# Values projected with 512 moving columns in two units ahead of the attention, and one filling tile per head

## The chip, the cores and the metric

The kernel runs on one core of one Trainium2 chip. A core has five engines with their own instruction streams: TensorE (PE: matmul, with its weight loads listed as PEld), VectorE (DVE), ScalarE (ACT), GpSimd (POOL) and SyncE (SP, which here issues most of the loads). The metric is the device time of one execution in microseconds (us).

## What is computed

One trunk layer on x of 512 tokens by 1024 features, all in float32 (cut to what matters here):

```python
xn = rmsnorm(x, g)
u = xn @ W_in                       # columns: q | k | v | rnn_x | rnn_gate | gate_A | gate_B, 1024 each
# A: 16 heads of 64; a query of chunk c reads the keys of chunks c-8 .. c (chunks of 64 tokens)
s = q @ k.T / 8 + bias[head, clipped distance];  s = where(valid, s, -1e30)
o = softmax(s) @ v
# B: causal convolution of width 4 -> RG-LRU scan, times gelu(rnn_gate)
yA, yB = o @ W_attn_out, B @ W_rnn_out
h = x + (sigmoid(gate_A) * yA + sigmoid(gate_B) * yB) @ W_o
h = h + (silu(hn @ W_g) * (hn @ W_u)) @ W_ffn_out     # hn = rmsnorm(h)
out = rmsnorm(h)
```

## The kernel before

**Products.** A value of float32 is kept as a pair of fp32r numbers, high part and rest. `mm3` (L71 to L78) makes one product of pairs with three matmuls: high by high (L76), high by low (L77), low by high (L78). `split` (L82, L83) makes a pair: ACT copies the high part out of the source, DVE subtracts it from the source. The stationary side of a matmul has 128 columns; the moving side has up to 512, and the result fills up to 512 columns of one PSUM bank. There are eight banks: four for tiles of the kind "mm", two for "t", two for "s".

**Weights.** `plan` lists chunks of weights in the order in which they are loaded. SP loads them into a ring of raw buffers, and `weights(name)` returns a chunk as pairs and has the next one in the list split by ACT and DVE while PE uses this one.

**Stages.** The norm; then the projections of branch B and the gates; then q and k of the first pair of heads (`q_tile(0)`, `k_tile(0)`); then the stage in question; then `po_ya` (the attention's way out), the merge, `w_o` and the feed-forward part.

**Projections for attention.** Two heads share one tile of q and one of k (128 features by 512 tokens): 24 matmuls of 128x512 each, `project` calling `mm3` for eight slices of the features. `q_tile` (L834) evicts with two ACT (L841) and two DVE instructions (L842). `k_tile` (L845) evicts each half with ACT (L852), DVE (L853), ACT (L854), all reading the same bank, and POOL copies the low half (L855). Four heads share one group of values, 256 columns of the weights. `v_tile(group, t)` (L868) makes the values of 128 tokens: the tokens are the stationary side, the 256 weight columns the moving side, 24 matmuls of 128x256; one split evicts it.

**A head.** `scores(h)` (L879) makes four blocks of scores with eight matmuls (L895, L896) into an "s", an "mm" and an "s" bank; DVE adds the bias and takes the maximum (L904), ACT takes the exponential and its sum (L905), DVE the reciprocal (L906), POOL multiplies (L910; the widest block goes to DVE in some heads). `transposed(h)` (L913) turns the blocks with ten matmuls (L921) into two "t" banks and an "mm" bank, and three splits evict them. `weigh(h)` (L930) multiplies by the values with eight matmuls (L941) into an "mm" bank; ACT (L942) and DVE (L943) evict, and each second head splits the pair's result.

**Order.** In front of the loop: the four `v_tile`s of group 0, then eight tiles `po_yb` of branch B's way out, with `scores(0)` after the sixth. In the loop (L964 to L983) PE's order is the order of the program: the transposes of head h, the scores of head h + 1, filling tiles, the weighing of head h, further filling tiles. `laid(h)` (L953) is the table of the filling tiles: from head 0 to 11 it spreads the q and k tiles of later pairs and the values of the next group, three or four narrow tiles beside or in place of a wide one; heads 12 to 15 have one tile of gate A each. The other engines' order in this stage is made by a scheduler.

Of the kernel before, what the change touches and what calls it, by code (L numbers as in the profile page):

```python
# [8 lines left out]
F32 = mybir.dt.float32  # L9
F32R = mybir.dt.float32r  # L10
# [4 lines left out]
P = 128  # L15
D = 1024
S = 512
KT = D // P
NT = S // P
HEADS = 16  # L20
HD = 64
# [17 lines left out]
def block_kernel(ctx: ExitStack, tc: tile.TileContext, x, norm_mix_g, w_in, b_merge, rel_table,  # L39
# [31 lines left out]
    def mm_tile(name, tag="mm"):  # L71
        return ps.tile([P, S], F32, tag=tag, bufs=4 if tag == "mm" else 2, name=name)

    def mm3(o, sh, sl, mh, ml, start, stop, parts=False):

        pe.matmul(o, sh, mh, start=start, stop=False, skip_group_check=parts)  # L76
        pe.matmul(o, sh, ml, start=False, stop=False, skip_group_check=parts)  # L77
        pe.matmul(o, sl, mh, start=False, stop=stop, skip_group_check=parts)  # L78

    def split(hi, lo, src):  # L80

        act.activation(hi, src, AF.Copy)  # L82
        dve.tensor_sub(lo, src, f(hi))  # L83
# [5 lines left out]
    def cols(src, col, width=CW):  # L89
        return (src, col, width)  # L90
# [16 lines left out]
    def plan_qk(pr):  # L107
        plan(f"qk{pr}", cols(w_in, C_Q + pr * P, P), cols(w_in, C_K + pr * P, P))

    def plan_v(gr):  # L110
        plan(f"v{gr}", cols(w_in, C_V + gr * CW))

    plan_qk(0)
    plan_v(0)
    for j in range(0, KT, 2):
        plan(f"yb{j}", cols(w_rnn_out, j * P))
    for pr in range(1, HEADS // 2):
        plan_qk(pr)
        if pr in (2, 4, 6):
            plan_v(pr // 2)  # L120
    for j in (4, 6):
        plan(f"ga{j}", cols(w_in, C_GA + j * P))
    for j in range(0, KT, 2):
# [212 lines left out]
    def weights(name, ahead=1):  # L336
        prefetch(index[name] + 1 + ahead)
        if index[name] + 1 == len(made):
            low_parts()
        return made[index[name]]  # L340
# [431 lines left out]
        return po  # L772


    zs = [[zp.tile([P, 2, S], F32, name=f"z{w}{j}") for j in range(0, KT, 2)] for w in "ab"]
    ta, zB = ([t[j // 2][:, j % 2] for j in range(KT)] for t in zs)
# [57 lines left out]
    def q_tile(pr):  # L834
        po = mm_tile(f"po_q{pr}")
        project(po, weights(f"qk{pr}"), 0, xnT)
        q = qk_pool(pr).tile([P, 2, S], F32R, tag="qk", bufs=3, name=f"q{pr}")
        for e in range(2):
            own, other = halves(e)
            src = backwards(po[own, :])  # L840
            act.activation(blocks(q[own, e]), src, AF.Copy, scale=0.125)  # L841
            dve.scalar_tensor_tensor(blocks(q[other, e]), src, 0.125, blocks(f(q[own, e])), ALU.mult, ALU.subtract)  # L842
        qk[pr] = [q]

    def k_tile(pr):  # L845
        po = mm_tile(f"po_k{pr}")
        project(po, weights(f"qk{pr}"), 1, xnT)
        kh = qk_pool(pr).tile([P, 2, S], F32R, tag="qk", bufs=3, name=f"kh{pr}")
        kl = qk_pool(pr).tile([P, 2, S], F32R, tag="qk", bufs=3, name=f"kl{pr}")
        for e in range(2):  # L850
            own, other = halves(e)
            act.activation(kh[own, e], po[own, :], AF.Copy)  # L852
            dve.tensor_sub(kl[own, e], po[own, :], f(kh[own, e]))  # L853
            act.activation(kh[other, e], po[own, :], AF.Copy)  # L854
            pool.tensor_copy(kl[other, e], kl[own, e])  # L855
        qk[pr] += [kh, kl]
# [8 lines left out]

    vs = {}

    def v_tile(gr, t):  # L868
        wv = weights(f"v{gr}")
        po = mm_tile(f"po_v{gr}_{t}", "mm" if gr else "t")  # L870
        for k in range(KT):
            mm3(po[:, 0:256], xnT[k][:, 0, t * P:(t + 1) * P], xnT[k][:, 1, t * P:(t + 1) * P],
                wv(0, k, whole), wv(1, k, whole), k == 0, k == KT - 1)
        v = aw.tile([P, 2, 4, HD], F32R, tag="v", bufs=8, name=f"v{gr}_{t}")
        split(v[:, :, 0::3], v[:, :, 1:3], po[:, 0:256].rearrange("p (a b d) -> p a b d", a=2, b=2))
        vs.setdefault(gr, []).append(v)


    def scores(h):  # L879
        pr, e = divmod(h, 2)  # L880
        q, kh, kl = qk[pr]
        bias = bias_tile(h)
        lsum = cp.tile([P, NT], F32, tag="lsum", bufs=2, name=f"l{h}")
        nmax = cp.tile([P, NT], F32, tag="nmax", bufs=2, name=f"m{h}")
        rl = cp.tile([P, NT], F32, tag="rl", bufs=2, name=f"rl{h}")
        prob = [aw2.tile([P, (qb + 1) * P], F32, tag=f"p{qb}", name=f"p{h}_{qb}") for qb in range(NT)]

        low = ps.tile([P, S], F32, tag="s", bufs=2, name=f"s{h}_01")
        scs = [low[:, 0:P], low[:, 256:512], mm_tile(f"s{h}_2"), ps.tile([P, S], F32, tag="s", bufs=2, name=f"s{h}_3")]

        def products(qb):
            w = (qb + 1) * P
            sc = scs[qb][:, 0:w]
            qs = q[:, e, qb * P:(qb + 1) * P]
            pe.matmul(sc, qs, kh[:, e, 0:w], start=True, stop=False, skip_group_check=qb < 2)  # L895
# [10 lines left out]
        dve.reciprocal(rl[:], lsum[:])  # L906
        for qb in range(NT):

            eng = dve if qb == NT - 1 and h % 4 == 1 and h > 1 else pool
            eng.tensor_scalar(prob[qb][:], prob[qb][:], rl[:, qb:qb + 1], 1.0, ALU.mult, ALU.mult)  # L910
        return prob

    def transposed(h, prob):  # L913

        pp = [aw2.tile([P, 2, S], F32R, tag="pt", bufs=4, name=f"pp{h}_{i}") for i in range(3)]
        for i, kbs in enumerate(((0,), (1,), (2, 3))):
            pt = mm_tile(f"pT{h}_{i}") if i == 2 else ps.tile([P, S], F32, tag="t", bufs=2, name=f"pT{h}_{i}")
            for kb in kbs:
                for qb in range(kb, NT):
                    at = qb - min(kb, 2) if kb < 3 else 2  # L920
                    pe.transpose(pt[:, at * P:(at + 1) * P], prob[qb][:, kb * P:(kb + 1) * P], ident[:])  # L921
            n = (512, 384, 384)[i]
            split(pp[i][:, 0, 0:n], pp[i][:, 1, 0:n], pt[:, 0:n])
        return pp
# [25 lines left out]

    def laid(h):  # L953
        m, at = divmod(h, 4)
        qs, ks, va = (lambda pr: lambda: q_tile(pr)), (lambda pr: lambda: k_tile(pr)), (lambda t: lambda: v_tile(m + 1, t))
        if h >= 12:
            return [lambda: gate(0, h - 8)], []
        first_, second = 2 * m + 2, 2 * m + 3
        return {0: (([qs(1), ks(1)] if m == 0 else []) + ([] if m == 0 else [qs(first_)]), [qs(first_)] if m == 0 else []),
                1: ([ks(first_)], [va(0)]),  # L960
                2: ([va(1), va(2)], [va(3)]),
                3: ([qs(second)], [ks(second)])}[at]

    for t in range(NT):  # L964
        v_tile(0, t)
# [394 lines left out]
```

## Time and profile before

| what | us |
|---|---|
| median of three runs | 867.02 (867.0 to 867.12) |
| span of the profiled execution | 865.5 |
| first values matmul to first `po_ya` matmul | 185.23 to 431.14 |
| transposes of head 0 | 241.60 |

The profile lists, for one execution, what each engine did and when. The span runs from the first to the last instruction; it is the profiled execution's own time and lies 1.5 us below the median of the runs. Matmuls are pipelined on PE, so the listed length of one overlaps the next; the distance between two starts says what one costs. In the views by windows each row is one stretch: its limits and length, then the busy time of PE, PEld, DVE, ACT and POOL with the number of instructions, then the clock granted to TensorE (1.00 is full speed), the share of time in which the DMA engines were busy, and GB/s. In a timeline row the first number is the start, the second the length; in square brackets stands the idle time of the engine ahead of it and what ended it. In the list of waits of an engine the numbers are the total, how often, and the longest.

### The profile page before, as it was taken

The numbers are of one execution on the slowest core, as the hardware profiler recorded it, in microseconds if no ns is written. First come the engines' busy times: TensorE is split into PE (matmuls) and PEld (weight loads), VectorE is DVE, ScalarE is ACT, GpSimd is POOL, SyncE is SP. The second block draws the span as 40 slices with busy tenths as digits, with TensorE's granted clock in tenths as the row PEclk, the third lists the DMA queues.
The fourth block names the chain that finished last, engine by engine and source line by source line (L and its number), as shares of the span: only waits on it lengthen the run. The fifth ranks groups of instructions, "written<-read, shape, count | busy, mean of one in ns | idle before, by whom it ended". The sixth has DMA issues, their size and how long they took to land.

```text
span 865.5 us, 13353 instructions
## 1 busy us (share of the span) xinstructions
PE 856.4 (99%) x5130; PEld 761.1 (88%) x5130; DVE 600.9 (69%) x950; ACT 498.1 (58%) x878; POOL 95.2 (11%) x161
## 2 busy tenths in 40 slices
PE   9999999999999999999999999999999999999997
PEld 6988888888889889898888889999999999888885
DVE  5666656573456585766556556988888888698885
ACT  6595747752356585767633357555555556545434
POOL 2412111120112132221200000000000001000000
PEclk9999999999999999999999999999999999999999
DMA  9133232433323332232223712424333332437542
GB/s 289 57 119 106 68 120 76 123 98 98 109 88 95 81 103 74 81 113 64 74 76 121 266 51 72 145 79 131 109 98 98 99 98 85 148 100 227 185 134 97
DMA packets 88767, 96.39 MB, mean 111 GB/s; under 512 B 5784, under 2 KB 74992, under 8 KB 88704
## 3 DMA queue, kind: packets, MB, share of 16 engines
q1 hardware_dynamic: 87072, 92.03, 34.3%
q10 hardware_dynamic: 1232, 2.95, 0.9%
q8 instruction: 40, 0.66, 0.3%
q0 software_dynamic: 400, 0.57, 0.2%
q14 instruction: 23, 0.19, 0.1%
HBM read 93.39 MB, written 2.14 MB: 110 GB/s over the span
## 4 chain that ended last, share of the span: by engine, by line
PE 97%; DVE 1%; ACT 1%; DMA 0%; issue 0%; ACTq 0%; DVEq 0%
PE po_out L76 2%; PE po_out L77 2%; PE po_out L78 2%; PE o L941 2%; PE p_fu L78 2%; PE p_fg L78 2%; PE p_fg L77 2%; PE p_fg L76 2%; PE p_fu L76 2%; PE p_fu L77 2%; PE pT L921 2%; PE po_v L76 2%; PE po_v L78 2%; PE po_v L77 2%; PE po_gb L76 2%; PE po_xr L77 2%
## 5 line engine op out<-in xcount | busy, mean ns | idle before, releaser
L910 POOL TENSOR_SCALAR p<-p,rl 128x128 f32<-128x128 f32 (+3 forms) x61 | 34.9, 590 | 135.7 <-DVE rl L906 135.4
L905 ACT ACTIVATE p<-p,m 128x128 f32<-128x128 f32 (+1 forms) x64 | 35.7, 560 | 11.0 <-DVE m L904 10.8
L76 PE MATMUL po_v<-whl_v,xnT 128*128 128x256 f32 x128 | 36.5, 285 | 0.0
L78 PE MATMUL po_v<-whl_v,xnT 128*128 128x256 f32 x128 | 36.2, 283 | 0.0
L77 PE MATMUL po_v<-whl_v,xnT 128*128 128x256 f32 x128 | 36.2, 283 | 0.0
L1131 POOL TENSOR_TENSOR act_lo<-act,act_hi 128x1024 fp32r<-128x1024 f32 x1 | 2.4, 2405 | 300.7 <-ACT act_hi L1130 300.7
L76 PE MATMUL po_out<-whl_fo,act_hi 128*128 128x512 f32 (+1 forms) x80 | 30.8, 385 | 0.5 <-ACT c_u L370 0.5
L78 PE MATMUL po_out<-whl_fo,act_lo 128*128 128x512 f32 (+1 forms) x80 | 30.7, 384 | 0.0
L77 PE MATMUL po_out<-whl_fo,act_hi 128*128 128x512 f32 (+1 forms) x80 | 30.7, 384 | 0.0
L904 DVE CUSTOM_DVE_ANT_0 p<-s,bias 128x128 f32<-128x128 f32 (+1 forms) x64 | 29.1, 483 | 1.0 <-PE s L896 1.0
L83 DVE TENSOR_TENSOR whl_qk<-raw_qk,whl_qk 128x1024 fp32r<-128x1024 f32 x16 | 20.5, 1284 | 13.2 <-ACT whl_qk L82 13.0
L83 DVE TENSOR_TENSOR whl_fu_s<-s_fu,whl_fu_s 128x1024 fp32r<-128x1024 f32 x20 | 24.1, 1222 | 6.2 <-ACT whl_fu_s L82 6.2
L77 PE MATMUL po_xr<-xnT,whl_xr 128*128 128x512 f32 (+1 forms) x80 | 27.7, 353 | 0.0
L83 DVE TENSOR_TENSOR pp<-pT,pp 128x384 fp32r<-128x384 f32 (+1 forms) x48 | 27.5, 596 | 0.1
L77 PE MATMUL po_gr<-xnT,whl_gr 128*128 128x512 f32 (+1 forms) x80 | 27.5, 347 | 0.0
L78 PE MATMUL po_gr<-xnT,whl_gr 128*128 128x512 f32 (+1 forms) x80 | 27.3, 347 | 0.0
L78 PE MATMUL po_xr<-xnT,whl_xr 128*128 128x512 f32 (+1 forms) x80 | 27.2, 346 | 0.0
L76 PE MATMUL po_gr<-xnT,whl_gr 128*128 128x512 f32 (+1 forms) x80 | 27.2, 347 | 0.0
L83 DVE TENSOR_TENSOR whl_fg_s<-s_fg,whl_fg_s 128x1024 fp32r<-128x1024 f32 x20 | 24.0, 1222 | 4.1 <-ACT whl_fg_s L82 4.0
L76 PE MATMUL po_xr<-xnT,whl_xr 128*128 128x512 f32 (+1 forms) x80 | 26.3, 351 | 0.4 <-ACT xnT L566 0.4
L82 ACT ACTIVATE whl_qk<-raw_qk 128x1024 fp32r<-128x1024 f32 x16 | 16.8, 1053 | 17.0 <-PE po_yb L78 10.4
L76 PE MATMUL po_gb<-xnT,whl_gb 128*128 128x512 f32 x64 | 25.2, 394 | 0.0
(487 smaller groups left out, 3247.5 us busy)
## 6 DMA issues: line engine op xcount, KB each, us to landing
raw_fg<-in_w_ffn_in_dram SPq DMA_DIRECT2D x24, 512.0 KB, 4.2
raw_fu<-in_w_ffn_in_dram SPq DMA_DIRECT2D x22, 512.0 KB, 3.9
raw_qk<-in_w_in_dram SPq DMA_DIRECT2D x32, 256.0 KB, 3.2
raw_fo<-in_w_ffn_out_dram SPq DMA_DIRECT2D x16, 512.0 KB, 3.6
raw_xr<-in_w_in_dram SPq DMA_DIRECT2D x8, 512.0 KB, 4.3
raw_gr<-in_w_in_dram SPq DMA_DIRECT2D x8, 512.0 KB, 3.6
raw_ga<-in_w_in_dram SPq DMA_DIRECT2D x8, 512.0 KB, 4.7
raw_gb<-in_w_in_dram SPq DMA_DIRECT2D x8, 512.0 KB, 3.5
```

Source lines behind the costliest of these rows:

```text
L76: pe.matmul(o, sh, mh, start=start, stop=False, skip_group_check=parts)
L77: pe.matmul(o, sh, ml, start=False, stop=False, skip_group_check=parts)
L78: pe.matmul(o, sl, mh, start=False, stop=stop, skip_group_check=parts)
L82: act.activation(hi, src, AF.Copy)
L83: dve.tensor_sub(lo, src, f(hi))
L904: dve.tensor_tensor_reduce(prob[qb][:], scs[qb][:, 0:w], bias[:, S - w:S], -1.0, 3e38, ALU.add, ALU.min, nmax[:, qb:qb + 1])
L905: act.activation(prob[qb][:], prob[qb][:], AF.Exp, bias=nmax[:, qb:qb + 1], scale=-1.0, accum_out=lsum[:, qb:qb + 1])
L910: eng.tensor_scalar(prob[qb][:], prob[qb][:], rl[:, qb:qb + 1], 1.0, ALU.mult, ALU.mult)
L921: pe.transpose(pt[:, at * P:(at + 1) * P], prob[qb][:, kb * P:(kb + 1) * P], ident[:])
L941: pe.matmul(po[:, S - n:S], st, pp[i][:, part, lo:lo + n], start=kb == 0 and part == 0, stop=kb == NT - 1 and part == 1)
L1131: (dve if i else pool).tensor_sub(lo[:], o[:], f(hi[:]))
```

## The change

The values of all four groups are now made ahead of the loop, in two units of two groups each: (0, 3) and (1, 2). A unit has 512 moving columns, 256 of each group, and four PSUM banks at once, one for each block of 128 tokens. It takes its weights in two chunks, each with half of the features and 512 columns. PE goes through two slices of the features for one bank (six matmuls), then to the next bank. Each bank is evicted by two splits, one for each group. The groups 0 and 3 lie in the buffers that values had before; group 1 lies in a buffer of the ring that later takes the pairs of attention results, and group 2 in two buffers that later take gate A's last tiles (`z_tiles`).

In front of the loop now stand `v_unit(0)`, the eight `po_yb` tiles with `scores(0)` after the sixth, `q_tile(1)`, `k_tile(1)`, `v_unit(1)` and `scores(1)`. In the loop each head has one filling tile, right behind its transposes, and then come the scores of head h + 2.

```diff
-    def plan_v(gr):
-        plan(f"v{gr}", cols(w_in, C_V + gr * CW))
+    v_groups = ((0, 3), (1, 2))
+
+    def plan_v(u):
+        for kh in range(2):
+            plan(f"v{u}_{kh}", *(cols(w_in, C_V + gr * CW) for gr in v_groups[u]), rows=kh * S, kts=KT // 2)
...
-    for pr in range(1, HEADS // 2):
+    plan_qk(1)
+    plan_v(1)
+    for pr in range(2, HEADS // 2):
         plan_qk(pr)
-        if pr in (2, 4, 6):
-            plan_v(pr // 2)
...
-    def v_tile(gr, t):
-        wv = weights(f"v{gr}")
-        po = mm_tile(f"po_v{gr}_{t}", "mm" if gr else "t")
-        for k in range(KT):
-            mm3(po[:, 0:256], xnT[k][:, 0, t * P:(t + 1) * P], xnT[k][:, 1, t * P:(t + 1) * P],
-                wv(0, k, whole), wv(1, k, whole), k == 0, k == KT - 1)
-        v = aw.tile([P, 2, 4, HD], F32R, tag="v", bufs=8, name=f"v{gr}_{t}")
-        split(v[:, :, 0::3], v[:, :, 1:3], po[:, 0:256].rearrange("p (a b d) -> p a b d", a=2, b=2))
...
+    def v_unit(u):
+        po = [mm_tile(f"po_v{u}_{t}") for t in range(NT)]
+        for kh in range(2):
+            wv = weights(f"v{u}_{kh}")
+            for kk in range(0, 4, 2):
+                for t in range(NT):
+                    toks = slice(t * P, (t + 1) * P)
+                    for k in (kk, kk + 1):
+                        xk = xnT[4 * kh + k]
+                        mm3(po[t][:], xk[:, 0, toks], xk[:, 1, toks], wv(0, k, every), wv(1, k, every),
+                            kh == k == 0, kh == 1 and k == 3)
+        homes = [v_homes(gr) for gr in v_groups[u]]
+        for t in range(NT):
+            for n, gr in enumerate(v_groups[u]):
+                v = homes[n][t]
+                v = v[:] if gr in v_groups[0] else v
+                split(v[:, :, 0::3], v[:, :, 1:3],
+                      po[t][:, n * CW:(n + 1) * CW].rearrange("p (a b d) -> p a b d", a=2, b=2))
...
-    def laid(h):
-        m, at = divmod(h, 4)
...
+    def fill(h):
         if h >= 12:
-            return [lambda: gate(0, h - 8)], []
...
+            if h % 2 == 0:
+                z_tiles("a", (h - 8,))
+            return gate(0, h - 8)
+        (k_tile if h % 2 else q_tile)(2 + h // 2)
+
+    v_unit(0)
+    probs = {}
     for j in range(KT):
         if j == 6:
-            prob = scores(0)
+            probs[0] = scores(0)
...
+    q_tile(1)
+    k_tile(1)
+    v_unit(1)
+    probs[1] = scores(1)
     with tc.manual_schedule(engines={mybir.EngineType.PE}):
         for h in range(HEADS):
-            pp = transposed(h, prob)
-            if h + 1 < HEADS:
-                prob = scores(h + 1)
-            before, after = laid(h)
-            for what in before:
-                what()
+            pp = transposed(h, probs.pop(h))
+            fill(h)
+            if h + 2 < HEADS:
+                probs[h + 2] = scores(h + 2)
             weigh(h, pp)
-            for what in after:
-                what()
```

How PE's order stands before and after, at three places. In these rows a name carries a buffer number at its end; `po_v0_2` is the PSUM tile of group (before) or unit (after) 0 for the tokens of block 2, `whl_...` is the split weight. The first place is PE at the start of the values, before:

```order
L78 MATMUL po_k0_1669<-xnT_155,whl_qk0_4_1571 128x512
L76 MATMUL po_v0_0_1722<-whl_v0_0_1630,xnT_155 128x256
...
L76 MATMUL po_v0_0_1722<-whl_v0_4_1635,xnT_155 128x256
...
L76 MATMUL po_v0_1_1750<-whl_v0_0_1630,xnT_155 128x256
```

and after the change, each row being the first of six matmuls or more on the same bank (the fourth bank's tile, `po_v0_3`, comes 38 matmuls behind the first):

```order
L76 MATMUL po_v0_0_1712<-whl_v0_0_0_1628,xnT_155 128x512
...
L76 MATMUL po_v0_1_1713<-whl_v0_0_0_1628,xnT_155 128x512
...
L76 MATMUL po_v0_2_1714<-whl_v0_0_0_1628,xnT_155 128x512
...
L76 MATMUL po_v0_0_1712<-whl_v0_0_2_1634,xnT_155 128x512
...
L76 MATMUL po_v0_0_1712<-whl_v0_1_0_1716,xnT_155 128x512
L77 MATMUL po_v0_0_1712<-whl_v0_1_0_1716,xnT_155 128x512
L76 MATMUL po_v0_3_1715<-whl_v0_0_0_1628,xnT_155 128x512
```

Before, one narrow tile ran through all 24 matmuls on one bank; now four banks take turns, and the fourth begins late.

The second place is PE in head 5 (`pT` are the transposes, `s` the scores, `o` the weighing), before:

```order
L921 MATMUL pT5_0_2859<-ident_119,p5_0_2776 128x128
...
L895 MATMUL s6_01_2888<-kh3_2738,q3_2695 128x128
...
L76 MATMUL po_k4_2912<-xnT_155,whl_qk4_0_2659 128x512
...
L941 MATMUL o5_2947<-pp5_0_2856,v1_0_2447 128x512 x2
...
L76 MATMUL po_v2_0_2973<-whl_v2_0_2805,xnT_155 128x256
...
L921 MATMUL pT6_0_3004<-ident_119,p6_0_2884 128x128
```

and after the change, with the semaphores that the rows wait for:

```order
L953 MATMUL pT5_0_2940<-ident_119,p5_0_2786 128x128 [waits PE_49,Pool_49]
...
L76 MATMUL po_k4_2959<-xnT_155,whl_qk4_0_2636 128x512 [waits DVE_49]
...
L927 MATMUL s7_01_3004<-kh3_2770,q3_2672 128x128
...
L973 MATMUL o5_3028<-pp5_0_2937,v1_2343 128x512 [waits DVE_49,Activation_49]
...
L953 MATMUL pT6_0_3045<-ident_119,p6_0_2897 128x128 [waits PE_49,Pool_49]
...
L76 MATMUL po_q5_3064<-xnT_155,whl_qk5_0_2850 128x512 [waits DVE_49]
```

The k tile of pair 4 moved ahead of the scores, the scores are those of head 7 where they were those of head 6, the values tile behind the weighing is gone, and the q tile that follows in head 6 waits for DVE.

More of the change, by code (lines that the diff above doesn't have):

```diff
@@ L772, in tile_of, with z_tiles @@
         return po
-    zs = [[zp.tile([P, 2, S], F32, name=f"z{w}{j}") for j in range(0, KT, 2)] for w in "ab"]
-    ta, zB = ([t[j // 2][:, j % 2] for j in range(KT)] for t in zs)
+    def z_tiles(w, js):
+        for j in js:
+            late = w == "a" and j >= 4
+            t = zp.tile([P, 2, S], F32, tag="late" if late else f"z{w}{j}", bufs=2 if late else 1, name=f"z{w}{j}")
+            for c in range(2):
+                (ta if w == "a" else zB)[j + c] = t[:, c]
+    ta, zB = {}, {}
+    z_tiles("a", (0, 2))
+    z_tiles("b", range(0, KT, 2))
     def gate(w, j):
@@ L866, in block_kernel, with v_homes @@
     vs = {}
-    def v_tile(gr, t):
-        wv = weights(f"v{gr}")
-        po = mm_tile(f"po_v{gr}_{t}", "mm" if gr else "t")
-        for k in range(KT):
-            mm3(po[:, 0:256], xnT[k][:, 0, t * P:(t + 1) * P], xnT[k][:, 1, t * P:(t + 1) * P],
-                wv(0, k, whole), wv(1, k, whole), k == 0, k == KT - 1)
-        v = aw.tile([P, 2, 4, HD], F32R, tag="v", bufs=8, name=f"v{gr}_{t}")
-        split(v[:, :, 0::3], v[:, :, 1:3], po[:, 0:256].rearrange("p (a b d) -> p a b d", a=2, b=2))
-        vs.setdefault(gr, []).append(v)
+    def v_homes(gr):
+        if gr in v_groups[0]:
+            return [aw.tile([P, 2, 4, HD], F32R, tag="v", bufs=8, name=f"v{gr}_{t}") for t in range(NT)]
+        if gr == v_groups[1][0]:
+            big = rnp.tile([P, 2, 2, S], F32R, tag="big", bufs=4, name=f"v{gr}")
+            rows = [big[:, t // 2, t % 2] for t in range(NT)]
+        else:
+            pairs = [zp.tile([P, 2, S], F32R, tag="late", bufs=2, name=f"v{gr}_{n}") for n in range(2)]
+            rows = [pairs[t // 2][:, t % 2] for t in range(NT)]
+        return [o.rearrange("p (a b d) -> p a b d", a=2, b=4) for o in rows]
+    def v_unit(u):
[16 more added lines that the diff above has]
+                      po[t][:, n * CW:(n + 1) * CW].rearrange("p (a b d) -> p a b d", a=2, b=2))
+                vs.setdefault(gr, []).append(v)
     def scores(h):
@@ L949, in weigh @@
             aT.append(o)
-    def laid(h):
-        m, at = divmod(h, 4)
-        qs, ks, va = (lambda pr: lambda: q_tile(pr)), (lambda pr: lambda: k_tile(pr)), (lambda t: lambda: v_tile(m + 1, t))
+    def fill(h):
         if h >= 12:
-            return [lambda: gate(0, h - 8)], []
[L958 to L965, printed above, removed]
+            if h % 2 == 0:
[4 more added lines that the diff above has]
+    probs = {}
     for j in range(KT):
         if j == 6:
-            prob = scores(0)
+            probs[0] = scores(0)
         po = mm_tile(f"po_yb{j}")
```

## The prediction

> **What bounds the kernel now.** I read the busy times of the engines first, then the chain of waits that ended last, then what PE (TensorE) waited for over the whole program.
>
> ```profile
> PE 856.4 (99%) x5130; PEld 761.1 (88%) x5130; DVE 600.9 (69%) x950; ACT 498.1 (58%) x878; POOL 95.2 (11%) x161
> PE 97%; DVE 1%; ACT 1%; DMA 0%; issue 0%; ACTq 0%; DVEq 0%
> PE busy L396 <- DVE eps_t L402: 1.2, 1, 1.2
> PE pt_mix_0t L564 <- DVE xs_mix L544: 0.6, 2, 0.4
> PE po_out L76 <- ACT c_u L370: 0.5, 1, 0.5
> PE po_xr L76 <- ACT xnT L566: 0.4, 2, 0.2
> ```
>
> PE is busy for 856.4 of the 865.5 us, 97% of the chain is PE, and its listed waits (the last four rows: total, times, longest) belong to the warm-up, the first norm, the first projection and the last stage. None names a tile of the attention. The windows over the stretch that the change touches, from the first values matmul to the last head's end, say the same; two more of them serve below.
>
> ```profile
> 185.23:241.60 56.37, 56.37 (x297) 48.70 (x296) 23.22 (x34) 18.39 (x28) 5.12 (x8) 1.00 0.33 98
> 241.60:431.14 189.54, 189.54 (x1129) 169.33 (x1128) 125.84 (x273) 125.81 (x273) 44.76 (x84) 1.00 0.30 86
> 348.27:366.42 18.15, 18.15 (x102) 15.86 (x100) 13.81 (x33) 14.42 (x33) 4.75 (x9) 1.00 0.30 88
> 405.19:414.27 9.08, 9.08 (x53) 7.92 (x52) 5.38 (x14) 6.35 (x15) 3.30 (x6) 1.00 0.01 3
> 742.15:745.80 3.65, 3.65 (x18) 3.01 (x17) 3.25 (x3) 1.33 (x2) 0.00 (x0) 1.00 0.38 140
> ```
>
> The columns are length, then busy us of PE, PEld, DVE, ACT and POOL, then the granted clock, the DMA share and GB/s. PE fills both stretches to the last digit (56.37 of 56.37, 189.54 of 189.54) at a clock of 1.00. So there is no wait in here to remove: only less PE work can shorten it, and any new PE wait lengthens it one for one.
>
> **The term that shrinks: values at half the instructions.** A busy time on PE overlaps its neighbours, so I price by spacing of starts, not by the mean duration.
>
> ```profile
> L76 PE MATMUL po_v<-whl_v,xnT 128*128 128x256 f32 x128 | 36.5, 285 | 0.0
> 174.35 0.39 PE L76 MATMUL po_q<-xnT,whl_qk 128*128 128x512 f32 x1
> 185.23 0.28 PE L76 MATMUL po_v<-whl_v,xnT 128*128 128x256 f32 x1
> 275.92 0.28 PE L76 MATMUL po_v<-whl_v,xnT 128*128 128x256 f32 x1
> 281.67 0.40 PE L941 MATMUL o<-pp,v 128*128 128x512 f32 x1
> ```
>
> Between 174.35 and 185.23 stand the 48 wide matmuls of q0 and k0: 10.88/48 = 0.2267 us each. Between 275.92 and 281.67 stand the 48 narrow ones of two values tiles: 5.75/48 = 0.1198 us. The difference, 0.1069 us for 256 more columns, is 0.418 ns a column; what is left of the narrow one, 0.1198 − 0.1069 = 0.0129 us, is paid once per matmul whatever its width. The values take 3 × 128 = 384 narrow matmuls now and 192 wide ones after, so 384 × 0.1198 = 46.0 us become 192 × 0.2267 = 43.5 us: **2.5 us less**. The row 742.15:745.80 shows wide matmuls in the shape of the new unit, whose PSUM bank changes after every six:
>
> ```profile
> 742.15 0.40 PE L76 MATMUL po_out<-whl_fo,act_hi 128*128 128x512 f32 x1
> 743.54 0.39 PE L76 MATMUL po_out<-whl_fo,act_hi 128*128 128x512 f32 x1
> 744.90 0.39 PE L76 MATMUL po_out<-whl_fo,act_hi 128*128 128x512 f32 x1
> ```
>
> They start 1.39 and 1.36 us apart, 0.232 and 0.227 us per matmul. With 0.232 throughout the unit would cost 1.0 us more; with the 0.2267 of the long stretch, nothing. I take the 0.2267, since the second group is already back at it, and keep a gain of 1.5 to 2.5 us. The trace has no wide matmul with tokens as the stationary and weights as the moving side; its worst would be twice the narrow spacing, 0.2396 us, at which the gain is 0.
>
> Here the Trainium skill speaks against the change: TensorE: Matmul & The Clock Gate, section Back-to-back issue gap, gives an isolated warm matmul N/2.4 + 2.5 ns. By its 2.5 ns the saving would be 192 × 2.5 ns = 0.5 us, an estimate from that page, and the time about 866.5 us. The trace's 12.9 ns is five times that, and it also disagrees with the same section's sustained 131 ns for N=512, being 227 ns here; I go by the trace.
>
> **What moves at no PE work.** Outside that, PE does the same matmuls in another order: per head ten transposes, one filling tile, eight score matmuls, eight weighing matmuls. The seams between kinds could cost. A head of that content exists already, with scores ahead of the filler (head 13), and one with the filler straight behind the transposes (head 15, which has no scores left):
>
> ```profile
> 405.19 1.28 PE L921 MATMUL pT<-ident,p 128*128 128x128 f32 x10
> 407.59 0.40 PE L76 MATMUL po_ga<-xnT,whl_ga 128*128 128x512 f32 x1
> 413.06 1.37 PE L941 MATMUL o<-pp,v 128*128 128x512 f32 x8
> 423.34 1.28 PE L921 MATMUL pT<-ident,p 128*128 128x128 f32 x10
> 424.38 0.48 PE L76 MATMUL po_ga<-xnT,whl_ga 128*128 128x512 f32 x1
> 429.93 1.37 PE L941 MATMUL o<-pp,v 128*128 128x512 f32 x8
> 431.14 0.44 PE L76 MATMUL po_ya<-aT,whl_ya 128*128 128x512 f32 x1
> 229.43 0.22 PE L895 MATMUL s<-kh,q 128*128 128x128 f32 x1
> 230.70 0.40 PE L76 MATMUL po_yb<-rnn,whl_yb 128*128 128x512 f32 x1
> ```
>
> Head 15 gives transposes 1.04, filler 5.55, weighing 1.21; scores behind wide matmuls took 230.70 − 229.43 = 1.27. The sum for the new order is 9.07 us, against 9.08 for head 13. So the seams are worth 0, with ±0.05 a head over 14 heads, ±0.7 us, kept for the range.
>
> **What the other engines are asked.** The scores of a head now come two heads ahead of its transposes. Softmax ends on POOL:
>
> ```profile
> 411.21 3.02 POOL L910 TENSOR_SCALAR p<-p,rl 128x128 f32<-128x128 f32 x4 [5.23 <-DVE rl L906]
> ```
>
> These end at 414.23, and the next head's transposes start at 414.27 (407.59 + 5.47 + 1.21): just in time, with the scores one head ahead. Two heads ahead they have another 9.07 us. Since PE did not wait for them, that is worth 0 now, but it is the cover for the rest: from the end of the scores (407.59) to POOL's end (414.23) lie 6.64 us, and the new place of the scores behind the filler leaves only the weighing's 1.21 us between them and the next transposes. With scores one head ahead in that place PE would lose 5.4 us a head.
>
> The new order has one q or k tile in every head from 0 to 11. The window 348.27:366.42 is exactly such a pair, two heads with one k and one q tile between them: ACT 14.42 and DVE 13.81 of 18.15 us, 79% and 76%, and PE did not wait. It holds a weight split of values that the new loop lacks, so the new loop is not denser than this. The narrow values' evictions, four for every four heads, leave the loop too and go to the two units in front:
>
> ```profile
> L82 ACT ACTIVATE v<-po_v x16: 361/384/385, 189.1 to 381.8; 128x256 fp32r<-128x256 f32 x16
> L83 DVE TENSOR_TENSOR v<-po_v,v x16: 417/424/427, 189.9 to 382.6; 128x256 fp32r<-128x256 f32 x16
> ```
>
> A unit holds four banks and each needs two of these pairs: 2 × 0.384 + 0.424 = 1.19 us. Within a unit the banks finish one after the other, 6 × 0.2267 = 1.36 us apart, so the first is free 4.08 − 1.19 = 2.9 us ahead of the unit's end and the last 1.19 us behind it. What follows wants banks of that kind one by one. Worth 0; if ACT were held up until a unit's end, each unit would cost one bank's 1.19 us, 2.4 us for both. At the front the unit needs four banks at once and the k tile ahead of it holds one; the built order starts the fourth tile only after 38 matmuls, 8.6 us into the unit.
>
> Loads: the same bytes in the same half-megabyte portions, 3 of the 4 MB of values weights earlier, past the later q and k loads on SP's queue, in stretches where the DMA share is 0.33 and 0.30. Worth 0; weights are split one chunk ahead as before.
>
> **The sum.** 865.5 − 2.5 + 0 = 863.0 us of span. The median of the runs shown, 867.02, is 1.5 above the span, which I carry over: **864.5 us**. The low end is 0.7 less by seams (863.8); the high end takes the seams the other way (865.2).
>
> **The rivals.**
>
> *A: k-tile evictions become the stop (slower).* A k tile is evicted half by half, each on one bank in series ACT, DVE, ACT:
>
> ```profile
> L852 ACT ACTIVATE kh<-po_k x16: 591/593/596, 185.8 to 399.7; 64x512 fp32r<-64x512 f32 x16
> L853 DVE TENSOR_TENSOR kl<-po_k,kh x16: 682/686/695, 187.2 to 402.4; 64x512 fp32r<-64x512 f32 x16
> 348.47 0.59 ACT L852 ACTIVATE kh<-po_k 64x512 fp32r<-64x512 f32 x1 [1.67 <-PE po_k L78]
> 348.96 1.04 ACT L82 ACTIVATE whl_v<-raw_v 128x1024 fp32r<-128x1024 f32 x1
> 355.28 0.60 ACT L854 ACTIVATE kh<-po_k 64x512 fp32r<-64x512 f32 x1 [0.49 <-DVE kl L853]
> ```
>
> Dense, that is 4 × 0.593 + 2 × 0.686 = 3.74 us, and with one weight split (1.04) ahead of it in ACT's queue 4.8; in the trace it stretched from 348.47 to 355.88, 7.4 us, since nobody waited. From a k tile's end to the next filler PE has scores, weighing and transposes, 1.27 + 1.21 + 1.04 = 3.5 us. If the next filler takes the k tile's bank, PE loses at least 1.3 us, and 3.9 by the stretched chain. I take 1.5 in six heads, 9 us: 864.5 + 9 = 873.5. For it: the order now puts fillers closer to evictions than before. Against it: the built program makes the filler behind a k tile wait on DVE alone, which is the reader of a score tile; the k tile's last reader is ACT. It decides if the banks go round so that a filler meets the k tile's own.
>
> *B: the gain is eaten (no change).* Either the two evictions show, 864.5 + 2.4 = 866.9, or the wide form with moving weights runs at the bound of 0.2396 us, which gives 867.0; the skill's rule above is its mild form. For it: that form is not in the trace. Against it: the narrow form moves weights as well, and PEld, which loads the stationary side, is busy for 88% against PE's 99%, so the loads are hidden as they stand.
>
> *C: the clock.* If the units' bank changes made the granted clock drop to half, each wide matmul would cost 512 × 0.418 ns = 0.214 us more: 192 × 0.214 = 41 us, about 905. Against it: 742.15:745.80 changes banks the same way at 1.00. The Trainium skill, same page, section A second HAM failure mode: psum-queue depth-cycling, tells of such an oscillation when banks are cycled; this trace disagrees at that place, with its 1.00.
>
> *D: "two heads ahead" brings a gain of its own.* There is none to bring: PE has no idle time in 241.60:431.14.
>
> **How the numbers follow.** Forecast 0.70, B 0.16, A 0.11, C 0.03. Predicted is the likeliest, 864.5, whose own range is 863.8 to 865.2. To hold 8 in 10 it must take in B: 863.6 to 867.0 leaves out A and C, 0.14, and little else. What this measurement can tell from no change is 0.2%, 1.7 us: faster is below 865.3, slower above 868.7. The forecast lies wholly on the faster side (0.70), B in between (with a little from A's mild form: 0.17), A and C beyond (0.13).
>
> **What would show it.** Right: 192 wide values matmuls at starts 0.227 us apart; two units of 21.8 us each; heads 1 to 13 of 9.07 us from transposes to transposes; PE idle nowhere between the first unit and the last head. Wrong: a start of a q tile that waits for ACT behind a k tile (A); a wait at the first matmul behind a unit, or wide values matmuls at 0.24 us (B); a clock below 1.00 in the units (C). What would make the whole sum wrong is a PE wait of over 0.2 us in each head, which costs more than the 2.5 us saved.

## The result, and the profile after

| | before | after |
|---|---|---|
| median of six runs, us | 867.05 (867.0 to 867.12) | 864.38 (864.24 to 864.52) |
| span of the profiled execution, us | 865.5 | 862.8 |

The changed kernel takes 0.9969 of the time before, with a 95% interval of 0.9958 to 0.9980: 2.7 us less. Engine sums and the chain by engine from the page of the kernel after, and then what PE waited for over the whole program (total, times, longest, in us):

```profile
PE 853.1 (99%) x4938; PEld 750.9 (87%) x4938; DVE 601.8 (70%) x950; ACT 497.5 (58%) x878; POOL 95.9 (11%) x161
PE 97%; DVE 1%; ACT 1%; DMA 0%; issue 0%; ACTq 0%; DVEq 0%
```

```profile
PE busy L399 <- DVE eps_t L405: 1.2, 1, 1.2
PE pt_mix_0t L567 <- DVE xs_mix L547: 1.1, 2, 0.9
PE po_out L76 <- ACT c_u L373: 0.5, 1, 0.5
PE po_xr L76 <- ACT xnT L569: 0.4, 2, 0.2
```

There are 192 matmuls fewer (5130 to 4938), and the waits are at the same four places; none lies in the stage that was rewritten. The windows of that stage, and one of a pair of heads with a k and a q tile:

```profile
185.32:207.08 21.76, 21.76 (x98) 18.02 (x97) 9.66 (x13) 8.73 (x14) 2.92 (x3) 1.00 0.39 120
207.08:428.42 221.34, 221.34 (x1138) 190.01 (x1136) 139.77 (x294) 134.60 (x287) 48.16 (x89) 1.00 0.30 87
349.29:367.44 18.15, 18.15 (x103) 15.88 (x102) 14.66 (x35) 14.59 (x34) 6.20 (x11) 1.00 0.32 88
```

PE fills each to the last digit at a clock of 1.00. The stage as a whole, from the first values matmul to the first `po_ya` matmul, went from 185.23:431.14 to 185.32:428.40, that is from 245.91 to 243.08 us: 2.8 us less. What lies ahead and behind is as it was (0.1 us later at the start, 434.4 us from there to the end in both). In the timeline of PE the units and the heads read so:

```profile
185.32 0.39 PE L76 MATMUL po_v<-whl_v,xnT 128*128 128x512 f32 x1
207.08 0.22 PE L927 MATMUL s<-kh,q 128*128 128x128 f32 x1
262.76 0.39 PE L76 MATMUL po_v<-whl_v,xnT 128*128 128x512 f32 x1
284.52 0.22 PE L927 MATMUL s<-kh,q 128*128 128x128 f32 x1
349.29 1.28 PE L953 MATMUL pT<-ident,p 128*128 128x128 f32 x10
358.37 1.28 PE L953 MATMUL pT<-ident,p 128*128 128x128 f32 x10
367.44 1.28 PE L953 MATMUL pT<-ident,p 128*128 128x128 f32 x10
428.40 0.44 PE L76 MATMUL po_ya<-aT,whl_ya 128*128 128x512 f32 x1
```

Each unit lasts 21.76 us, 0.2267 us for each of its 96 matmuls, and a head 9.08 and 9.07 us from transposes to transposes.

### The profile page after: what moved, and what is told of

The parts are those of the page before. It is cut to its first block, busy times and chain, and to the rows that moved or that the text cites. A ratio compares the mean times of both kernels' runs of the same rounds, so it can differ in the third digit from the quotient of the medians.

```text
span 862.8 us, 13012 instructions
## 1 busy us (share of the span) xinstructions
PE 853.1 (99%) x4938; PEld 750.9 (87%) x4938; DVE 601.8 (70%) x950; ACT 497.5 (58%) x878; POOL 95.9 (11%) x161
## 4 chain that ended last, share of the span: by engine, by line
PE 97%; DVE 1%; ACT 1%; DMA 0%; issue 0%; ACTq 0%; DVEq 0%
PE po_out L76 2%; PE po_out L78 2%; PE po_out L77 2%; PE o L973 2%; PE p_fu L78 2%; PE p_fg L78 2%; PE p_fg L77 2%; PE p_fg L76 2%; PE p_fu L76 2%; PE p_fu L77 2%; PE pT L953 2%; PE po_gb L76 2%; PE po_xr L77 2%; PE po_xr L76 2%; PE po_ga L78 2%; PE po_k L76 2%
## 5 line engine op out<-in xcount | busy, mean ns | idle before, releaser
L942 POOL TENSOR_SCALAR p<-p,rl 128x128 f32<-128x128 f32 (+3 forms) x61 | 37.6, 636 | 91.1 <-DVE rl L938 85.9
L936 DVE CUSTOM_DVE_ANT_0 p<-s,bias 128x128 f32<-128x128 f32 (+2 forms) x64 | 28.7, 486 | 12.1 <-PE s L928 9.9
L937 ACT ACTIVATE p<-p,m 128x128 f32<-128x128 f32 (+2 forms) x64 | 35.6, 557 | 2.5 <-DVE m L936 2.2
L76 PE MATMUL po_k<-xnT,whl_qk 128*128 128x512 f32 x64 | 25.5, 398 | 0.0
L76 PE MATMUL po_q<-xnT,whl_qk 128*128 128x512 f32 x64 | 25.5, 398 | 0.0
L76 PE MATMUL po_ga<-xnT,whl_ga 128*128 128x512 f32 x64 | 25.4, 397 | 0.0
```

## Experiments

Every kernel here was timed against the kernel before, on the chip it ran on; the kernel before had 867.12 to 867.20 us there.

**1. The price of narrow matmuls.** The new order with the units made of matmuls of half the width (the edit below is the second version's). In the first version both halves of a bank started their accumulation, so that the first products of one half are dropped from the values; the second version starts once.

```diff
-                    for k in (kk, kk + 1):
-                        xk = xnT[4 * kh + k]
-                        mm3(po[t][:], xk[:, 0, toks], xk[:, 1, toks], wv(0, k, every), wv(1, k, every),
-                            kh == k == 0, kh == 1 and k == 3)
+                    for n in range(2):
+                        at = slice(n * CW, (n + 1) * CW)
+                        for k in (kk, kk + 1):
+                            xk = xnT[4 * kh + k]
+                            mm3(po[t][:, at], xk[:, 0, toks], xk[:, 1, toks], wv(0, k, at), wv(1, k, at),
+                                kh == k == n == 0, kh == n == 1 and k == 3, parts=True)
```

> The changed kernel with its two units and its new order, but each unit's 96 matmuls of 128x512 made as 192 of 128x256 on the same banks (384 in both, as before the change). Theory (a fixed 12.9 ns for each matmul, the order worth nothing): 192 x 0.0129 = 2.5 us are given back, 866.9 us. Rival (the gain comes from the new order): stays at 864.4. Rival (a fixed 2.5 ns): 864.9.

> Again the changed kernel with each unit's 96 wide matmuls made as 192 of 128x256, now with one start of accumulation per bank (the run before this one started each half of a bank by itself, which drops the first products of the other half). Theory (12.9 ns fixed): 866.9, as that run had it. Rival (the dropped products changed the time): off by more than 0.3.

Measured: 866.89 and 866.85 us (0.9996 of the kernel before, interval 0.9987 to 1.0005, both times). The rivals had 864.4 and 864.9. With 384 narrow matmuls again, the new order has the time of the old one; the gain is in the width. The second version's second unit, its first matmul and what follows it in the timeline, and then its window:

```profile
263.77 0.28 PE L76 MATMUL po_v<-whl_v,xnT 128*128 128x256 f32 x1
286.80 0.22 PE L929 MATMUL s<-kh,q 128*128 128x128 f32 x1
```

```profile
263.77:286.72 22.95, 22.95 (x193) 22.95 (x192) 8.56 (x11) 8.60 (x14) 1.22 (x2) 1.00 0.40 114
```

192 matmuls in 23.03 us, 0.1199 us each, against 21.76 us for the wide unit. The window also shows something that the prediction had not used: PEld, the weight loads, is busy for 22.95 of 22.95 us, where the wide unit has 18.02 of 21.76. So the extra may be the loads showing rather than a fixed part of each matmul, but the full column does not show it: a load is listed with 0.19 us, and here one starts every 0.12 us, so the listed loads overlap and fill the stretch whatever sets the pace. Both accounts give the same 2.5 us for this change.

**2. The same price with q and k.** Here the weights are the stationary side. A first version dropped products of one half in the same way, of q and k. The edit: `project` makes each slice in two halves of 256 tokens for q and k tiles.

```diff
+            for i, (a, b) in enumerate(((lo, (lo + hi) // 2), ((lo + hi) // 2, hi)) if narrow else ((lo, hi),)):
-            mm3(o[:, lo:hi], whl(0, k, at), whl(1, k, at),
-                xs[k][:, 0, lo:hi], xs[k][:, 1, lo:hi], k == 0, k == n - 1)
+                mm3(o[:, a:b], whl(0, k, at), whl(1, k, at),
+                    xs[k][:, 0, a:b], xs[k][:, 1, a:b], k == i == 0, k == n - 1 and i == narrow, parts=narrow)
...
-        project(po, weights(f"qk{pr}"), 0, xnT)
+        project(po, weights(f"qk{pr}"), 0, xnT, narrow=True)
```

> The changed kernel with its 16 q and k tiles made by 48 matmuls of 128x256 instead of 24 of 128x512: 384 matmuls more, here with the weights as the stationary side. Theory (the fixed 12.9 ns belong to every matmul): 384 x 0.0129 = 5.0 us, 869.3 us. Rival (a fixed 2.5 ns, or a price of the values' form alone): 865.3 or less.

> Again the changed kernel with q and k tiles made of matmuls of 128x256, with one start of accumulation per bank. Theory (12.9 ns fixed for every matmul): 384 x 0.0129 = 5.0 us, 869.3; the run before had 869.15. Rival: off by more than 0.5.

Measured: 869.15 and 869.20 us (1.0023, interval 1.0015 to 1.0032, for the second). That is 4.8 us above the changed kernel for 384 matmuls more, 12.5 ns each. From experiment 1 it is (866.85 − 864.38)/192 = 12.9 ns. These differences cross chips; with each run taken against the kernel before on its own chip (2.67 us below it for the changed kernel, 0.31 below and 2.04 above it for the narrow ones) both come to 12.3 ns. The price does not belong to the values or to which side is stationary.

**3. The bank changes.** The unit goes to the next bank after three matmuls, and after twelve, in place of six (`for kk in range(4)` with one slice, and one pass with four).

> The changed kernel with the unit's bank changed after every three matmuls instead of six: 32 changes more in the two units. Theory (a bank change costs PE nothing): 864.4, within 0.3. Rival (the 0.03 us by which one group of six in the last stage was longer is the price of a change): 865.4, with starts in the units 0.237 us apart in the mean.

> The changed kernel with the unit's bank changed after every twelve matmuls. Theory (a bank change costs nothing; only the spacing of the banks' ends matters, here 2.7 us against 1.19 us of eviction): 864.4, within 0.2, and no wait behind the units. Rival (each change costs a little): 863.9.

Measured: 865.04 us (0.9975, 0.9965 to 0.9984) and 864.40 us (0.9969, 0.9956 to 0.9981). Neither theory had 865.04. In the run with changes after three, the second unit and what follows it read:

```profile
263.81 0.39 PE L76 MATMUL po_v<-whl_v,xnT 128*128 128x512 f32 x1
285.58 0.93 PE L953 MATMUL pT<-ident,p 128*128 128x128 f32 x7
287.61 0.47 PE L76 MATMUL po_q<-xnT,whl_qk 128*128 128x512 f32 x1 [0.42 <-DVE m L936]
```

The unit takes 21.77 us, so a change costs nothing. But the order at the unit's end came out otherwise (six score matmuls stand ahead of the unit that stood behind it), and the first q tile behind it waits 0.42 us for a bank that DVE still reads. The run with changes after twelve has no such wait and the time of the changed kernel.

**4. What the bank of the filler is worth (rival A, made to happen).** All q and k tiles of the loop share one PSUM bank.

```diff
+    held_bank = []
+    def one_bank(pr):
+        if pr >= 2 and not held_bank:
+            held_bank.append(mm_tile("po_qk"))
+        return held_bank[0] if pr >= 2 else None
...
-        po = mm_tile(f"po_q{pr}")
+        po = one_bank(pr) or mm_tile(f"po_q{pr}")
...
-        po = mm_tile(f"po_k{pr}")
+        po = one_bank(pr) or mm_tile(f"po_k{pr}")
```

> The changed kernel with the q and k tiles of the loop all in one PSUM bank, so that a q tile behind a k tile must wait for the k tile's last eviction on ACT (five places), and a k tile for the q tile's (six places, two pairs of ACT and DVE, some 2.6 us dense). Theory (the k tile's serial evictions are harmless only because the next filler takes another bank): five waits of 1.3 us at least (a dense chain) up to 4.4 us (the chain of 356.07 to 363.79 in the changed kernel against the next filler at 359.41): 871 to 886, likeliest 875. Rival (the evictions come in time whatever the bank): 864.4 to 865.

Measured: 900.20 us (1.0381, 1.0365 to 1.0396), 36 us above the changed kernel: above both. PE's waits, one place in the timeline, and the windows: the first from the transposes ahead of that place to its end, the other five from the end of each long wait to the return of the full clock:

```profile
PE po_qk L76 <- ACT kh L871: 20.8, 5, 4.2
PE po_qk L76 <- DVE q L859: 2.0, 6, 0.3
```

```profile
309.97 0.80 PE L76 MATMUL po_qk<-xnT,whl_qk 128*128 128x512 f32 x1 [4.17 <-ACT kh L871]
```

```profile
304.52:309.97 5.45, 1.28 (x13) 1.04 (x12) 4.91 (x9) 5.32 (x14) 1.97 (x6) 0.84 0.72 188
309.97:315.05 5.08, 5.08 (x12) 4.02 (x13) 1.13 (x2) 0.47 (x1) 1.08 (x2) 0.50 0.02 4
335.52:338.95 3.43, 3.43 (x8) 2.76 (x9) 1.14 (x2) 0.46 (x1) 0.87 (x2) 0.50 0.00 1
360.26:366.25 5.99, 5.99 (x14) 4.79 (x15) 1.06 (x2) 0.47 (x1) 1.03 (x2) 0.50 0.00 0
386.26:390.15 3.89, 3.89 (x10) 3.06 (x11) 0.93 (x2) 0.47 (x1) 0.55 (x1) 0.56 0.00 0
411.04:414.04 3.00, 3.00 (x7) 2.42 (x8) 1.07 (x2) 0.47 (x1) 1.03 (x2) 0.50 0.00 0
```

Five waits of 4.2 us on ACT, as the stretched chain had it (4.4), and six short ones. What the expectation had not counted stands in the five windows: behind each of these waits the granted clock was about 0.5, for 3.0 to 6.0 us. At half the clock half of such a stretch is lost, 1.5 to 3.0 us, 10.5 us in all. With some 4.4 us for each wait itself (from the end of the transposes, 304.52 + 1.03, to 309.97), one costs 5.9 to 7.4 us and the five 32.5. The six short ones add 2.0 us as listed, which leaves 1 of the 35.5 us between the spans (898.3 and 862.8).

**5. The distance of the scores, in the new place.** One head ahead, behind the filler (`scores(h + 1)` where `scores(h + 2)` stood, and no `scores(1)` ahead of the loop).

> The changed kernel with the scores one head ahead instead of two, left in their new place behind the filling tile. Theory (two heads ahead is the cover for that place): from the scores' end to the next transposes only the weighing's 1.21 us are left against 6.64 us of softmax, so 5.4 us of PE wait in each of 15 heads, 81 us: 945 us (930 to 990). Rival (the distance doesn't matter, another engine's slack carries it): 864 to 870.

Measured: 955.59 us (1.1027, 1.1006 to 1.1048), 91 us more, 6.1 us for each of 15 heads against 5.4 expected. The wait is where it was placed; the window behind it holds the heads that wait:

```profile
PE pT L953 <- POOL p L942: 51.9, 40, 4.9
```

```profile
293.00:511.00 218.00, 164.63 (x723) 133.84 (x722) 102.40 (x237) 106.77 (x237) 41.58 (x82) 0.84 0.17 50
```

51.9 us are listed as waits on the softmax's last step, 3.5 us for each of 15 heads and not 5.4. The spans differ by 87.8 us (950.6 and 862.8), so 36 us are something else. Most of it is the clock: in these heads its mean was 0.84, and 16% of the 164.63 us in which PE was busy is 26 us, an estimate that takes the clock as the same in busy and idle time. So the expectation came near in sum, with a wait that was too long and a clock that its sum did not count.

**6. The distance in the old place.** One head ahead and in front of the filler, which is the old loop's order with one filler for each head.

```diff
             pp = transposed(h, probs.pop(h))
-            fill(h)
-            if h + 2 < HEADS:
-                probs[h + 2] = scores(h + 2)
+            if h + 1 < HEADS:
+                probs[h + 1] = scores(h + 1)
+            fill(h)
             weigh(h, pp)
```

> The changed kernel with the scores one head ahead instead of two, and in front of the filling tile: transposes(h), scores(h+1), filler(h), weighing(h). Theory (two heads ahead is worth nothing by itself, since from the scores' end to the next transposes lie 5.45 + 1.21 = 6.7 us, as long as the softmax takes): 864.4, at most 865.5 where ACT's evictions of k tiles push the softmax back. Rival (the earlier scores are part of the gain): 866 or more, with PE waits for POOL at the transposes.

Measured: 871.95 us (1.0055, 1.0042 to 1.0068), 7.6 us above the changed kernel: the theory fell, the rival's side is right.

```profile
PE pT L953 <- POOL p L942: 2.2, 9, 0.3
PE po_q L76 <- DVE oacc L975: 1.4, 5, 0.3
PE po_ga L76 <- DVE oacc L975: 0.3, 1, 0.3
```

```profile
304.57 0.40 PE L928 MATMUL s<-kl,q 128*128 128x512 f32 x1
305.27 0.50 PE L76 MATMUL po_q<-xnT,whl_qk 128*128 128x512 f32 x1 [0.30 <-DVE oacc L975]
305.61 0.39 PE L77 MATMUL po_q<-xnT,whl_qk 128*128 128x512 f32 x1
```

Fifteen short waits, 3.9 us as listed. They cost more than is listed: the matmul behind the one at 305.27 would have started at 304.57 + 2 × 0.2267 = 305.02 and starts at 305.61, 0.59 us late for a listed 0.30. A part of that is how idle time is listed: it counts from the listed end of the matmul before, 0.40 us behind its start, where the next one would have started after 0.2267. Fifteen times 0.3 us beside the listed 3.9 make 8.4, against 7.4 in the spans (870.2 and 862.8). The waits for the bank of the weighing stand at five q tiles and one gate tile; those for POOL stand at the transposes that follow these six heads.

**7. The distance alone, in the kernel before.** Scores two heads ahead in the old loop with its narrow values: first right behind the transposes (in head 0 behind its first filling tiles), then, since that run showed a wait of its own, behind the fillers. Both make `scores(1)` ahead of the loop. The second version's loop:

```diff
-            pp = transposed(h, prob)
-            if h + 1 < HEADS:
-                prob = scores(h + 1)
+            pp = transposed(h, probs.pop(h))
             before, after = laid(h)
             for what in before:
                 what()
+            if h % 4 and h + 2 < HEADS:
+                probs[h + 2] = scores(h + 2)
             weigh(h, pp)
             for what in after:
                 what()
+            if h % 4 == 0 and h + 2 < HEADS:
+                probs[h + 2] = scores(h + 2)
```

> The kernel before the change, narrow values in the loop as they were, with the scores two heads ahead alone. Theory (PE waited for nothing there, so the distance brings nothing by itself): 867.0, within 0.5. Rival (the distance is a gain of its own): 866 or less.

> The kernel before the change, narrow values in the loop, scores two heads ahead, but now behind the head's first filling tiles (in heads 0, 4, 8 and 12 behind the weighing), so that none of them follows straight on the k tile that it reads. Theory (the loss of the run before, 13.7 us, was four waits for a k tile just made; the distance itself is worth nothing): 867.0 to 867.6 and no wait of PE on ACT's kh. Rival (the distance itself costs, through buffers that are held longer): 870 or more.

Measured: 880.80 us (1.0156, 1.0142 to 1.0169) for the first, a miss on both sides, and 867.31 us (1.0001, 0.9992 to 1.0010) for the second. The first run's waits, and windows of some 5 us behind each of the four places:

```profile
PE s L895 <- ACT kh L854: 9.4, 4, 2.4
```

```profile
257.30:262.50 5.20, 5.20 (x28) 4.57 (x29) 3.75 (x12) 3.83 (x11) 1.02 (x3) 1.00 0.54 158
307.85:313.00 5.15, 5.15 (x19) 4.50 (x20) 3.76 (x13) 3.34 (x10) 0.66 (x2) 0.70 0.39 119
359.78:365.00 5.22, 5.22 (x25) 4.49 (x26) 3.77 (x13) 3.34 (x10) 0.61 (x1) 1.00 0.38 120
410.27:415.50 5.23, 5.23 (x19) 4.55 (x20) 3.77 (x13) 3.35 (x10) 0.73 (x2) 0.70 0.31 100
```

In heads 0, 4, 8 and 12 the scores read a k tile whose evictions were not done: one wait of 2.2 us and three of 2.4 us. Behind the first and the third the clock stayed at 1.00, behind the second and the fourth it was 0.70, though the last three are equally long: the length alone did not decide. With the scores behind the fillers the wait is gone and the time is the old one. So the distance as such brings nothing to the kernel before, and costs nothing.

**8. The place of the scores in the changed kernel.** Two heads ahead, in front of the filler instead of behind it.

> The changed kernel with the scores of head h + 2 in front of the filling tile instead of behind it. For each even head from 0 to 10 they then read a k tile that ended only a weighing and ten transposes earlier, 1.21 + 1.04 us. Theory (the k tile's evictions are what the place behind the filler covers): waits of PE on kh in six heads (five where k1, made ahead of the loop, is ready), at 3.4 us each by the run with four of them (13.7 / 4): 881 to 885. Rival (the place doesn't matter): 864.4 to 865.

Measured: 868.89 us (1.0020, 1.0011 to 1.0029), 4.5 us above the changed kernel. The place of the wait is as expected, its size is not.

```profile
PE s L927 <- ACT kh L865: 2.4, 6, 0.4
PE po_q L76 <- DVE m L936: 0.2, 1, 0.2
```

```profile
306.01 0.33 PE L927 MATMUL s<-kh,q 128*128 128x128 f32 x1 [0.40 <-ACT kh L865]
```

Six heads wait, 0.4 us each, with no drop of the clock in a pair of such heads; the price of 3.4 us, taken from long waits of which two slowed the clock, does not carry over. A seventh wait of 0.2 us stands at a q tile. With 0.3 us for each beside the 2.6 us that are listed, as in experiment 6, the seven make 4.7 us, against 4.3 in the spans (867.1 and 862.8).

This run and that of experiment 6 differ in the distance alone (and in `scores(1)` ahead of the loop): both have the scores in front of the filler, one head ahead takes 871.95 us and two take 868.89. So in the changed kernel the distance is worth 3.1 us there, though it was worth nothing in the kernel before.

## Why the prediction was right

**The bound and the term.** That PE alone sets the time of this stage, and that the width saves 192 times 12.9 ns, was right: experiments 1 and 2 give the 2.5 us back and find the same price at another place. The stage itself shrank by 2.8 us; 0.3 us of it is not in the width (866.85 with narrow units against 867.16 before, within the interval of no change). That is inside the 0.7 us kept for the seams, and a head came out at the 9.07 us that the prediction added up. The 1.39 us for one group of six in the last stage was not the price of a bank change, as the choice of 0.2267 had it; experiment 3 has units of 21.77 us with twice the changes. The prediction's own range, 863.8 to 865.2, held the seams alone; the 1.0 us that it kept for a wider spacing was not in it and was not needed.

**What the price is.** The prediction read a part that every matmul pays whatever its width. The runs bear that out between 256 and 512 columns only. Two score matmuls of 384 columns, which lie between, take 293.17 − 292.82 = 0.35 us, 0.175 each, where 12.9 ns and 384 times 0.418 ns make 0.173: in keeping, as far as rows of 0.01 us tell.

```profile
292.82 0.34 PE L927 MATMUL s<-kh,q 128*128 128x384 f32 x1
293.17 0.39 PE L927 MATMUL s<-kh,q 128*128 128x512 f32 x1
350.32 0.48 PE L76 MATMUL po_k<-xnT,whl_qk 128*128 128x512 f32 x1
```

At 128 columns it fails: ten transposes take 350.32 − 349.29 = 1.03 us, 0.103 each, where the sum would be 0.066. So there is some floor for narrow forms. Whether the 0.12 us of 256 columns are such a floor too, set by the weight loads, or a sum was not tried; the saving is the same either way.

**Rival A.** Its condition did not occur: the built order gives the filler behind a k tile another bank. Its size was wrong by much. The prediction took 1.5 us a place, from a chain of evictions run densely, and kept 3.9 as the far bound; made to happen, the place costs 5.9 to 7.4 us, the clock included. The traces show why a dense chain was the wrong row: ACT takes other work between the steps. The first two rows are the changed kernel's, the third is experiment 4's, where ACT works in the same way although PE waits.

```profile
356.07 0.59 ACT L863 ACTIVATE kh<-po_k 64x512 fp32r<-64x512 f32 x1 [1.66 <-PE po_k L78]
363.19 0.60 ACT L865 ACTIVATE kh<-po_k 64x512 fp32r<-64x512 f32 x1
309.32 0.59 ACT L871 ACTIVATE kh<-po_qk 64x512 fp32r<-64x512 f32 x1
```

From the first step's start to the last one's end lie 7.7 us, while the next filler starts at 359.4. In experiment 4 the chain ends at 309.91, and the filler starts at 309.97.

**Rival B** did not occur: the wide form with moving weights has the spacing of the others, and nothing waits behind the units. Experiment 3 shows how near it is: with another order at a unit's end, one wait costs 0.7 us. The reason that the prediction gave against it was weak: the 88% of PEld is the mean of the whole program, and in the narrow stretch that the prediction itself timed, the loads are busy for 5.75 of 5.75 us, which by itself shows neither that they are hidden nor that they are not.

```profile
275.92:281.67 5.75, 5.75 (x49) 5.75 (x48) 3.55 (x11) 3.22 (x11) 1.96 (x4) 1.00 0.18 46
```

**Rival C** did not occur in the units (clock 1.00). **Rival D** fell as argued for the kernel before: experiment 7 has 867.31.

**The cover.** That two heads ahead brings nothing to the kernel before and carries the new place of the scores was right, and the 5.4 us a head were near in sum (6.1). It was said too narrowly: by the 6.68 us that head 13 left against 6.64, the old place with one head ahead seemed good as well, and experiment 6 shows that it is not, by 7.6 us. Head 13 has a gate for filler. In a head with a q tile behind one with a k tile, the softmax stands in line with other work, as DVE and POOL of experiment 6 show:

```profile
302.88 1.61 DVE L83 TENSOR_TENSOR whl_qk<-raw_qk,whl_qk 128x1024 fp32r<-128x1024 f32 x1 [0.27 <-ACT whl_qk L82]
304.52 0.69 DVE L975 TENSOR_TENSOR oacc<-o,oacc 64x512 f32<-64x512 f32 x1
305.25 0.29 DVE L936 CUSTOM_DVE_ANT_0 p<-s,bias 128x128 f32<-128x128 f32 x1
309.87 0.17 DVE L938 RECIPROCAL rl<-l 128x4 f32<-128x4 f32 x1
311.21 2.06 POOL L942 TENSOR_SCALAR p<-p,rl 128x128 f32<-128x128 f32 x4
```

The scores began at 303.45. DVE's first maximum comes at 305.25, behind a weight split and the eviction of the weighing, and POOL ends at 313.27, 8.5 us after the end of the scores (304.57 + 0.23) and not 6.64. So 0.04 us was no margin. The pair of heads 348.27:366.42, which the prediction took as proof that the new loop is not denser, has the same tiles, the same length and one head ahead, and PE did not wait there; why that pair was spared was not taken apart. Over the whole loop the heads before the change were longer, since the values stood between them, and that this was the slack is likely but not shown.

## What to carry to other kernels

Where PE never waits, a tile made with half as many matmuls of twice the width (512 columns for 256) saves a fixed amount for each one removed, which two spacings of the old trace give ahead of time. Moving PE work out of a loop can use up the time in which other engines hid: the order has to be loosened in the same step, here by making scores a head earlier and by keeping each consumer a full tile behind the evictions that it reads; with either left out, the new loop lost 4.5 us or more. A wait priced by a dense chain is too cheap if the engine does other work in between, and a long wait can cost half the clock behind it as well.

## What the runs showed of the hardware

Waits of PE cost more than is listed. Short ones (0.3 us listed) made the second matmul behind them 0.59 us late, of which 0.17 us is the part of the matmul before that the next would have overlapped. Behind all five waits of 4.2 us the granted clock was about 0.5, for 3.0 to 6.0 us; behind a wait of 2.2 us it stayed at 1.00, and behind three of 2.4 us it stayed once at 1.00 and was twice 0.70 over 5.2 us. The Trainium skill, TensorE: Matmul & The Clock Gate, section HAM oscillation — how this bites in real kernels, says that PE idle gaps of more than about 3.4 us bring the clock down. The 4.2 us gaps agree; two of the three gaps of 2.4 us show that here a shorter one can do it too.

The same page of the Trainium skill, section Back-to-back issue gap, holds that the spacing of matmuls is set by the weight load and the matmul together. The narrow unit is in keeping with that but does not show it, since its listed loads overlap; no run here changes the load alone.
